# A two-layer hybrid decoder trunk on one core: the order of the first loads, weight splits and row factors

## The chip, the cores and the metric

The kernel runs on one core of a Trainium2 chip. A core has a matrix engine (TensorE, "PE" in the profile; its weight loads are listed apart as "PEld"), three engines for elementwise work (VectorE "DVE", ScalarE "ACT", GpSimd "POOL"), a queue engine (SyncE "SP") and 16 DMA engines that all queues share. Each engine runs its own list of instructions in the order in which the program was built; semaphores make one engine wait for another. The metric is the device time of one execution in microseconds, the median over runs. Lower is better.

## The reference

The input `x` has 256 rows of 1024 float32 values. Two layers follow each other; each adds half a SwiGLU, a token mixer and again half a SwiGLU, and a last norm closes:

```python
for layer in range(DEPTH):
    x = x + 0.5 * swiglu(rmsnorm(x, ffn1_norm[layer]), ffn1_w_gu[layer], ffn1_w_down[layer])
    h = rmsnorm(x, mix_norm[layer])
    y = gated_deltanet(h, ...) if layer % 2 == 0 else sliding_window_attention(h, ...)
    x = x + y
    x = x + 0.5 * swiglu(rmsnorm(x, ffn2_norm[layer]), ffn2_w_gu[layer], ffn2_w_down[layer])
return rmsnorm(x, final_norm)

def rmsnorm(x, w):
    return x * rsqrt(mean(x * x, axis=-1) + 1e-6) * w
def swiglu(h, w_gu, w_down):            # w_gu: 1024 x 5632, w_down: 2816 x 1024
    gate, up = split(h @ w_gu, 2)
    return (silu(gate) * up) @ w_down
```

## The kernel before

`x` stays on the chip as two row blocks of 128 rows (`t` = 0 and 1). The weights stream in from memory once, as float32, in pieces of 512 KB. float32 accuracy comes from three fast products: every operand is split into a high part with fewer bits and the rest. For a weight piece, `split` (L262) fetches `raw` on SP's queue, copies it into the reduced type on ACT (`whi`, L275), and subtracts that on DVE (`wlo`, L276). `mm3` (L306) then issues hi·hi, hi·lo and lo·hi; in the rows of the matrix engine these are L309 to L311. There are four buffers for `raw` and five each for `whi` and `wlo`, handed out in turn: the fifth `raw` can only be fetched when the first has been split, and the sixth `whi` can only be written when the products with the first are done.

`ffn` (L330) goes through the 2816 columns in eleven steps `c` of 256. Each step takes four pieces: two for the gate columns (`wg`: rows 0 to 511 and 512 to 1023 of `w_gu`) and two for the up columns (`wu`). A step has 4 products of 8 inner tiles each, so 96 matrix instructions. From step 1 on they are in the transposed form (`proj_T`), with both row blocks at once.

The very first norm is special (`First`, L125). The factor of a row, one over its root mean square, is not known when the first products could start. So the first step's products take `x * w` without the factor (`hh0`, `hl0`), one product for each row block, and the factor `r` is multiplied in behind (L372 to L374). `raw(t)` (L139) makes these operands: eight transposes of `x` on the matrix engine (`psT`, L149), a product with the norm's weights on DVE (`f`, L152), a copy of the high part on ACT (`hh`, L155) and a subtraction on DVE (`hl`, L156), in two halves `q` of four inner tiles. `factor(t)` (L159) takes squares and their sums on ACT (L164), and the power on POOL (L168). `scale()` (L172) spreads the factors over all partitions with two small products on the matrix engine (`prb<-dr,ones`, L177), copies the result on ACT (`rb`, L179), multiplies `f` by it on POOL in four parts (L183), and splits each part again (`hh` L185, `hl` L186). From step 1 on the products read these scaled operands.

Before the first data arrive, `warm` (L250) lets the matrix engine run products that nobody reads. After the transposes of row block 0, eight more of them follow (16 matrix instructions).

Three fetches go through ACT's queue at the start: `w8` (the first norm's weights, 4 KB), `nw` (the second norm's weights, spread over 128 partitions, 512 KB; used at the end of the first `ffn`) and `sk` (8 KB, used in the second layer). On SP's queue the order is: row block 0 of `x`, the two `wg` pieces, row block 1, the two `wu` pieces, and then the pieces of step 1 as buffers come free.

The order of instructions on each engine is not that of the Python code. A scheduler replays the program with estimated durations while it is built, and writes each engine's list in the order in which its instructions become ready there. `issue_after(ins)` tells it to put what follows behind `ins`. `hold` does that for the splits of a few weight pieces after a norm: their ACT and DVE instructions go behind the norm's last split.

## Time and profile before

| what | value |
|---|---|
| three runs | 1046.29, 1048.04, 1051.45 us; median 1048.04 us |
| span of the profiled execution | 1048.2 us |
| instructions in it | 18944 |
| read from memory | 174.92 MB, 168 GB/s over the span |
| DMA queue of SP: share of the 16 engines' time | 52.6% |
| ACT casts of weight pieces (L275) | 316, 1051 ns each on average |
| DVE subtractions of weight pieces (L276) | 302, 1268 ns each on average |

The profiled execution's own time, taken as its span, lies 0.2 us above the median of the three runs.

How to read the profile. A row of a timeline has the start in us, the time from the first to the last end of what is merged in it, the engine, the source line, the operation, `out<-in` by the program's names, the sizes and the count. In square brackets stand the idle time of the engine before it and what ended that. Matrix instructions are pipelined, so each lasts longer than the distance to the next start; the rate is read from starts. `PEclk` is the share of its full clock that the matrix engine was granted. The buffer numbers are left out of names in the profile, so `hh` can be `hh0` of the first step (L155) or the scaled `hh` (L185), and `w` is the norm's row `w8`.

### The profile page before, as it was taken

The numbers are of one execution on the slowest core, as the hardware profiler recorded it, in microseconds if no ns is written. First come the engines' busy times: TensorE is split into PE (matmuls) and PEld (weight loads), VectorE is DVE, ScalarE is ACT, GpSimd is POOL, SyncE is SP. The second block draws the span as 40 slices with busy tenths as digits, with TensorE's granted clock in tenths as the row PEclk, the third lists the DMA queues.
The fourth block names the chain that finished last, engine by engine and source line by source line (L and its number), as shares of the span: only waits on it lengthen the run. The fifth ranks groups of instructions, "written<-read, shape, count | busy, mean of one in ns | idle before, by whom it ended". The sixth has DMA issues, their size and how long they took to land.

```text
span 1048.2 us, 18944 instructions
## 1 busy us (share of the span) xinstructions
PE 1021.5 (97%) x7683; PEld 956.2 (91%) x7683; DVE 625.9 (60%) x887; ACT 498.8 (48%) x847; POOL 220.4 (21%) x197
## 2 busy tenths in 40 slices
PE   8999999999979999999999999999999999999997
PEld 7999998899979889999988999998899689999986
DVE  5755554666895665565545655554568856555544
ACT  5544443557755544443434433444456644344432
POOL 3123410006743201122100022120021401221100
PEclk9999999999989999999999999999999999999999
DMA  7666666654442335566565566567653426655661
GB/s 225 188 192 186 183 213 190 186 156 130 133 141 83 120 101 162 161 187 200 195 195 179 173 190 190 163 195 217 215 180 123 133 89 191 201 172 173 212 196 43
DMA packets 135003, 177.20 MB, mean 169 GB/s; under 512 B 6930, under 2 KB 119940, under 8 KB 134916
## 3 DMA queue, kind: packets, MB, share of 16 engines
q1 hardware_dynamic: 131712, 171.46, 52.6%
q10 hardware_dynamic: 3204, 4.53, 1.4%
q8 instruction: 60, 0.98, 0.4%
q14 instruction: 27, 0.22, 0.1%
HBM read 174.92 MB, written 1.05 MB: 168 GB/s over the span
## 4 chain that ended last, share of the span: by engine, by line
PE 62%; issue 1%; DVE 1%; ACT 0%; POOLq 0%; POOL 0%; ACTq 0%
PE acc L311 7%; PE acc L309 7%; PE acc L310 7%; PE pg L309 6%; PE pg L311 6%; PE pu L311 6%; PE pu L309 6%; PE pu L310 6%; PE pg L310 6%; PE pq L309 1%; PE pq L311 1%; PE pq L310 1%; PE psc L1103 1%; PE po L1147 1%; PE psT L89 1%
## 5 line engine op out<-in xcount | busy, mean ns | idle before, releaser
L275 ACT CAST whi<-raw 128x1024 fp32r<-128x1024 f32 x316 | 330.0, 1051 | 313.9 <-PE pg L310 161.5
L276 DVE TENSOR_TENSOR wlo<-raw,whi 128x1024 fp32r<-128x1024 f32 x302 | 382.1, 1268 | 154.3 <-ACT whi L275 153.8
L389 POOL TENSOR_SCALAR ah<-act 128x256 fp32r<-128x256 f32 x80 | 103.5, 1294 | 389.9 <-DVE act L340 389.9
L310 PE MATMUL pg<-hl,whi 128*128 128x256 f32 x640 | 181.2, 283 | 1.0 <-DVE hl L186 1.0
L310 PE MATMUL pu<-hl,whi 128*128 128x256 f32 x640 | 181.3, 283 | 0.0
L311 PE MATMUL pg<-hh,wlo 128*128 128x256 f32 x640 | 181.2, 283 | 0.0
L309 PE MATMUL pu<-hh,whi 128*128 128x256 f32 x640 | 181.2, 283 | 0.0
L311 PE MATMUL pu<-hh,wlo 128*128 128x256 f32 x640 | 181.2, 283 | 0.0
L309 PE MATMUL pg<-hh,whi 128*128 128x256 f32 x640 | 181.1, 283 | 0.0
L310 PE MATMUL acc<-wlo,ah 128*128 128x512 f32 (+1 forms) x340 | 128.4, 378 | 0.0
L311 PE MATMUL acc<-whi,al 128*128 128x512 f32 (+1 forms) x340 | 128.2, 377 | 0.0
L309 PE MATMUL acc<-whi,ah 128*128 128x512 f32 (+1 forms) x340 | 127.9, 378 | 0.0
L310 PEld LDWEIGHTS pg<-hl,whi 128*128 128x128 f32 x640 | 122.9, 192 | 1.2 <-DVE hl L186 1.2
L311 PEld LDWEIGHTS pg<-hh,wlo 128*128 128x128 f32 x640 | 122.9, 192 | 0.0
L309 PEld LDWEIGHTS pg<-hh,whi 128*128 128x128 f32 x640 | 122.9, 192 | 0.0
L311 PEld LDWEIGHTS pu<-hh,wlo 128*128 128x128 f32 x640 | 122.8, 192 | 0.0
L309 PEld LDWEIGHTS pu<-hh,whi 128*128 128x128 f32 x640 | 122.8, 192 | 0.0
L310 PEld LDWEIGHTS pu<-hl,whi 128*128 128x128 f32 x640 | 122.8, 192 | 0.0
L340 DVE TENSOR_TENSOR act<-sg,pu 128x256 f32<-128x256 f32 x86 | 35.9, 418 | 98.0 <-PE pu L311 96.2
L309 PEld LDWEIGHTS acc<-whi,ah 128*128 128x128 f32 x340 | 64.0, 188 | 11.9
L311 PEld LDWEIGHTS acc<-whi,al 128*128 128x128 f32 x340 | 63.9, 188 | 12.0
L310 PEld LDWEIGHTS acc<-wlo,ah 128*128 128x128 f32 x340 | 64.0, 188 | 11.7
(343 smaller groups left out, 1623.5 us busy)
## 6 DMA issues: line engine op xcount, KB each, us to landing
raw<-in_ffn_w_gu_dram SPq DMA_DIRECT2D x176, 512.0 KB, 4.9
raw<-in_ffn_w_down_dram SPq DMA_DIRECT2D x88, 512.0 KB, 4.3
raw<-in_a_w_in_dram SPq DMA_DIRECT2D x32, 512.0 KB, 4.5
raw<-in_b_w_in_dram SPq DMA_DIRECT2D x12, 512.0 KB, 4.9
raw<-in_a_w_out_dram SPq DMA_DIRECT2D x8, 512.0 KB, 3.9
raw<-in_b_w_out_dram SPq DMA_DIRECT2D x8, 512.0 KB, 3.8
nw<-in_ffn_norm_dram ACTq DMA_DIRECT2D x3, 512.0 KB, 4.1
x<-in_x_dram SPq DMA_DIRECT2D x2, 512.0 KB, 7.1
```

The lines of the kernel that those rows point to most:

```text
L89: last = nc.tensor.transpose(ps[:, i * P:(i + 1) * P], xn[:, s.start + i * P:s.start + (i + 1) * P], k.ident)
L275: nc.scalar.copy(hi, raw)
L276: (eng or nc.vector).tensor_tensor(out=lo, in0=raw, in1=hi.bitcast(F32), op=ALU.subtract)
L309: nc.tensor.matmul(out, lhsT=lh, rhs=rh, start=start, stop=False)
L310: nc.tensor.matmul(out, lhsT=lh, rhs=rl, start=False, stop=False)
L311: return nc.tensor.matmul(out, lhsT=ll, rhs=rh, start=False, stop=stop)
L340: ahead[1] = nc.vector.tensor_mul(a, sg, pu[:, :T])
L389: ahead[2] = nc.gpsimd.tensor_scalar(oh, a, 1.0, None, op0=ALU.mult)
L1103: nc.tensor.matmul(out, lhsT=qT[:, j, b * P:(b + 1) * P], rhs=kz[:, kv, :, kt * P:(kt + 1) * P], start=True, stop=True)
L1147: lastpo[0] = nc.tensor.matmul(po[64 * i:64 * i + 64, b * P:(b + 1) * P], lhsT=v[:, kt, kv * HD:(kv + 1) * HD], rhs=pT[:, b + kt, i, :], s ...
```

## The change

Five things are altered, all at the start of the program.

1. The second norm's weights (`nw`) are no longer fetched at the start, but at step 3 of the first `ffn`, behind the gate activation that is then the latest.
2. The two `wg` pieces of step 0 are loaded in two halves each (inner tiles 0-1 and 2-3 of a piece), and each half is split on its own: `cuts=2`.
3. `hold` is now also set by `raw(0)`: the splits of the two `wg` pieces go behind the last split of row block 0.
4. `raw(1)` is issued from within the loop over the first products, behind those of row block 0 with `wg`; the loop now runs over row blocks outside and halves of the inner tiles inside. `factor` and `scale` go behind the last split of row block 1.
5. The second group of unread products is six instead of eight (12 matrix instructions instead of 16).

```diff
 class Norm:
-    def __init__(self, kern, wrow):
+    def __init__(self, kern, wrow, later=False):
         self.k = kern
-        self.w = kern.n4([P, D], "nw")
-        kern.nc.scalar.dma_start(out=self.w, in_=wrow.partition_broadcast(P))
+        self.wrow = wrow
         self.hh = self.hl = None
+        if not later:
+            self.fetch()
+
+    def fetch(self):
+        self.w = self.k.n4([P, D], "nw")
+        self.k.nc.scalar.dma_start(out=self.w, in_=self.wrow.partition_broadcast(P))
...
 class First(Norm):
...
             oh = self.hh0[:, ks, ts]
-            nc.scalar.copy(oh, f)
-            nc.vector.tensor_sub(self.hl0[:, ks, ts], f, oh.bitcast(F32))
+            hi = nc.scalar.copy(oh, f)
+            lo = nc.vector.tensor_sub(self.hl0[:, ks, ts], f, oh.bitcast(F32))
+        if t == 0:
+            k.hold = [0, 2, hi, lo]
+        self.done = (hi, lo) if t else None
         return tr
...
-    def split(self, src, hi, lo, shape, eng=None):
+    def split(self, src, hi, lo, shape, eng=None, cuts=1):
         raw = self.wp.tile(shape, F32, tag="raw", name="raw", bufs=4)
-        nc.sync.dma_start(out=raw, in_=src)
+        n = shape[1] // cuts
+        parts = [slice(i * n, (i + 1) * n) for i in range(cuts)]
+        for c in parts:
+            nc.sync.dma_start(out=raw[:, c], in_=src[:, c])
...
-            nc.scalar.copy(hi, raw)
-            (eng or nc.vector).tensor_tensor(out=lo, in0=raw, in1=hi.bitcast(F32), op=ALU.subtract)
+            for c in parts:
+                nc.scalar.copy(hi[:, c], raw[:, c])
+                (eng or nc.vector).tensor_tensor(out=lo[:, c], in0=raw[:, c], in1=hi[:, c].bitcast(F32), op=ALU.subtract)
...
-            wg = self.wcols(w_gu, c * 256)
+            wg = self.wcols(w_gu, c * 256, cuts=2 if c == 0 and late is not None else 1)
             if c == 0 and late is not None:
                 late()
+            if c == 3 and fetch is not None:
+                with self.tc.issue_after(ahead[0].ins):
+                    fetch()
             wu = self.wcols(w_gu, DFF + c * 256)
...
                 for n, w in ((0, wg), (1, wu)):
-                    for ks in (range(0, 4), range(4, 8)):
-                        for t in range(NT):
-                            self.part_N(pgs[t][n][:, :T], w, t, nrm.hh0, nrm.hl0, ks)
-                for t in range(NT):
-                    nrm.factor(t)
-                nrm.scale()
+                    for t in range(NT):
+                        for ks in (range(0, 4), range(4, 8)):
+                            mm = self.part_N(pgs[t][n][:, :T], w, t, nrm.hh0, nrm.hl0, ks)
+                            if nrm.done is None:
+                                with self.tc.issue_after(mm.ins):
+                                    nrm.raw(1)
+                with ExitStack() as behind:
+                    for ins in nrm.done:
+                        behind.enter_context(self.tc.issue_after(ins.ins))
+                    for t in range(NT):
+                        nrm.factor(t)
+                    nrm.scale()
...
     with tc.issue_after(nrm.raw(0).ins):
-        K.warm(8)
+        K.warm(6)

     def late():
         load(1)
-        nrm.raw(1)
```

What the scheduler makes of it is seen in the lists of the engines, which name tiles with a number. First ACT at the start of the program, before. `hh0` is the high part of `x * w`; `whi_134` and `whi_140` are the `wg` pieces of step 0, `whi_163` and `whi_169` its `wu` pieces, and `whi_330` is the first piece of step 1.

```order
L275 CAST whi_134<-raw_136 128x1024
L155 CAST hh0_86<-f_85 128x4x128
L275 CAST whi_140<-raw_142 128x1024
L155 CAST hh0_86<-f_85 128x4x128
L164 ACTIVATE xn_284,ss_283<-x_81 128x512 x2
L275 CAST whi_163<-raw_165 128x1024
L155 CAST hh0_86<-f_85 128x4x128 x2
L275 CAST whi_169<-raw_171 128x1024
L179 COPY rb_298<-prb_291 128x256
L372 ACT_TABLE_LOAD
L372 ACTIVATE sg_312<-pg_175,r0_281 128x256
L275 CAST whi_330<-raw_332 128x1024
```

With the change ACT first makes both high parts of row block 0, then the four half pieces of `wg`, then the two `wu` pieces, and then come these rows. `whi_332`, `whi_338`, `whi_344` and `whi_350` are the four pieces of step 1, and `whi_468` is the first piece of step 2.

```order
L287 CAST whi_332<-raw_334 128x1024
L160 CAST hh0_86<-f_85 128x4x128 x2
L172 ACTIVATE xn_278,ss_277<-x_81 128x512 x2
L172 ACTIVATE xn_286,ss_285<-x_81 128x512 x2
L287 CAST whi_338<-raw_340 128x1024
L287 CAST whi_344<-raw_346 128x1024
L287 CAST whi_350<-raw_352 128x1024
L287 CAST whi_468<-raw_470 128x1024
L187 COPY rb_300<-prb_293 128x256
L394 ACT_TABLE_LOAD
L394 ACTIVATE sg_314<-pg_161,r0_283 128x256
L394 ACTIVATE sg_323<-pg_163,r1_291 128x256
```

The high parts of row block 1 stood behind three weight pieces; now they stand behind five, the last of them step 1's first. The copy of the spread factors (`rb`) stood behind step 0's last piece; now four pieces of step 1 and one of step 2 stand ahead of it too.

Second, the matrix engine behind the gate products of row block 0, before (`pg_175` is the gate product of row block 0 and `pg_177` that of row block 1; `pu_176` and `pu_178` are the up products):

```order
L311 MATMUL pg_175<-whi_140,hl0_87 128x256
L177 MATMUL prb_291<-dr_295,ones_75 128x128
L309 MATMUL pg_177<-whi_134,hh0_86 128x256
L310 MATMUL pg_177<-wlo_135,hh0_86 128x256
L309 MATMUL pu_176<-whi_163,hh0_86 128x256
```

And with the change, where `pg_161`, `pg_163` and `pu_162` have the same roles:

```order
L323 MATMUL pg_161<-whi_139,hl0_87 128x256
L321 MATMUL pg_163<-whi_130,hh0_86 128x256
L322 MATMUL pg_163<-wlo_131,hh0_86 128x256
L321 MATMUL pu_162<-whi_149,hh0_86 128x256
L322 MATMUL pu_162<-wlo_150,hh0_86 128x256
```

One of the two products that spread the factors (`prb`) is gone from here; in both lists two products of row block 1 stand ahead of the up products of row block 0. From the first of these two to the end of step 0 there are 72 products.

Third, the matrix engine at the end of step 0, before (`pg_354` is the first product of step 1):

```order
L309 MATMUL pu_178<-whi_169,hh0_86 128x256
L310 MATMUL pu_178<-wlo_170,hh0_86 128x256
L311 MATMUL pu_178<-whi_169,hl0_87 128x256
L309 MATMUL pg_354<-hh_88,whi_330 128x256
L310 MATMUL pg_354<-hl_89,whi_330 128x256
```

And with the change (`pu_164` is the last product of step 0, `pat` transposes step 0's result, `pg_356`, `pu_357`, `pg_412` and `pu_413` are the four products of step 1):

```order
L323 MATMUL pu_164<-whi_155,hl0_87 128x256
L185 MATMUL prb_293<-dr_294,ones_75 128x128
L185 MATMUL prb_293<-dr_297,ones_75 128x128
L400 MATMUL pat_318<-ident_70,act_316 128x128 x2
L321 MATMUL pg_356<-hh_88,whi_332 128x256
L321 MATMUL pu_357<-hh_88,whi_344 128x256
L321 MATMUL pg_412<-hh_88,whi_332 128x256
L400 MATMUL pat_327<-ident_70,act_325 128x128 x2
L321 MATMUL pu_413<-hh_88,whi_344 128x256
L322 MATMUL pg_356<-hl_89,whi_332 128x256
```

Both products that spread the factors now stand behind the last product of step 0, and the first transposes of its result ahead of step 1; before, step 1 followed step 0 directly and the transposes came in its middle. From there on the lists of all engines come to the same order within step 1 or 2, and nothing later differs but the one fetch of `nw` on ACT's queue at step 3.

More of the change, by code (lines that the diff above doesn't have):

```diff
@@ L325, in part_N, with ffn @@
             wh, wl = w(k, slice(0, 256))
-            self.mm3(out, hh[:, k, ts], hl[:, k, ts], wh, wl, k == 0, k == KT - 1)
-    def ffn(self, nrm, w_gu, w_down, after, mid=None, late=None, final=None):
+            mm = self.mm3(out, hh[:, k, ts], hl[:, k, ts], wh, wl, k == 0, k == KT - 1)
+        return mm
+    def ffn(self, nrm, w_gu, w_down, after, mid=None, late=None, final=None, fetch=None):
         nc = self.nc
```

13 lines of the change are left out of this document (7 added, 6 removed).

## The prediction

> **What bounds the kernel now.** I read the page first, then the matrix engine's waits, then the granted clock and the starts of the first 40 us. The page says that the matrix engine works almost without a break and that the chain that ends last runs on it.
>
> ```profile
> PE 1021.5 (97%) x7683; PEld 956.2 (91%) x7683; DVE 625.9 (60%) x887; ACT 498.8 (48%) x847; POOL 220.4 (21%) x197
> ...
> PE 62%; issue 1%; DVE 1%; ACT 0%; POOLq 0%; POOL 0%; ACTq 0%
> ```
>
> So the end moves by as much as the matrix engine's start of steady work moves. Its waits between 8 and 40 us are the first four rows here; the last row is the longest one from 40 to 280 us.
>
> ```profile
> PE pg L309 <- ACT hh L155: 1.2, 1, 1.2
> PE pg L310 <- DVE hl L186: 1.0, 1, 1.0
> PE pg L311 <- DVE hl L156: 0.8, 1, 0.8
> PE pg L310 <- DVE wlo L276: 0.4, 1, 0.4
> ...
> PE pvn L621 <- ACT vT L838: 0.5, 1, 0.5
> ```
>
> From 40 us on it waits for nothing longer than 0.5 us until the first mixer's tail, and the lists behind step 1 are the same in both versions. So I compare one point: the start of step 2. Its row, and those of the beginning:
>
> ```profile
> 10.96 0.39 PE L309 MATMUL pg<-whi,hh 128*128 128x256 f32 x1 [1.15 <-ACT hh L155]
> ...
> 27.04 0.28 PE L309 MATMUL pg<-hh,whi 128*128 128x256 f32 x1
> ...
> 29.00 0.39 PE L310 MATMUL pg<-hl,whi 128*128 128x256 f32 x1 [0.96 <-DVE hl L186]
> ...
> 34.72 0.28 PE L309 MATMUL pg<-hh,whi 128*128 128x256 f32 x1
> ...
> 40.48 0.28 PE L309 MATMUL pg<-hh,whi 128*128 128x256 f32 x1
> ```
>
> Step 0 ends and step 1 starts at 27.04; step 2 starts at 40.48. The 48 products from 34.72 to 40.48 give 0.12 us each. The clock (PEclk is the column with 1.00 or 0.50) is a second cost:
>
> ```profile
> 8.91:12.33 3.42, 1.67 (x10) 1.08 (x9) 1.91 (x3) 2.56 (x4) 0.00 (x0) 1.00 1.07 392
> 12.33:15.74 3.41, 2.84 (x13) 2.84 (x14) 2.37 (x4) 2.74 (x6) 0.55 (x1) 0.50 1.06 326
> 15.74:19.15 3.41, 3.41 (x30) 3.28 (x29) 3.05 (x5) 2.32 (x4) 0.00 (x0) 1.00 0.40 135
> ...
> 295.60:299.05 3.45, 0.00 (x0) 0.00 (x0) 3.45 (x5) 0.00 (x0) 1.34 (x2) 1.00 0.22 23
> 299.05:302.46 3.41, 1.06 (x5) 1.10 (x6) 3.41 (x9) 0.81 (x3) 0.00 (x0) 0.50 0.86 286
> 302.46:305.87 3.41, 3.41 (x18) 3.41 (x18) 3.41 (x7) 1.43 (x3) 0.47 (x1) 0.50 0.46 153
> ...
> 363.90:367.30 3.40, 1.58 (x14) 1.61 (x15) 2.23 (x10) 0.95 (x6) 1.91 (x2) 1.00 0.67 201
> 13.28 0.41 PE L309 MATMUL pg<-whi,hh 128*128 128x256 f32 x1
> 13.49 0.41 PE L310 MATMUL pg<-wlo,hh 128*128 128x256 f32 x1
> ```
>
> Stretches of 3.4 us are at half clock behind a stretch in which the engine was busy half the time or less (8.91 to 12.33, 295.60 to 302.46). A product then takes 0.21 us: each us at half clock loses 0.44.
>
> **The first products.** Row block 0 of `x` is there at 5.1:
>
> ```profile
> 5.11 0.63 ACT L164 ACTIVATE xn<-x 128x512 f32<-128x512 f32 x1 [1.54 <-DMA x<-in_x_dram]
> ...
> 5.13 1.97 PE L149 MATMUL psT<-ident,x 128*128 128x128 f32 x8 [0.40 <-DMA x<-in_x_dram]
> 6.89 2.91 PE L254 MATMUL warm<-ident 128*128 128x128 f32 x16
> ...
> 9.34 1.04 ACT L275 CAST whi<-raw 128x1024 fp32r<-128x1024 f32 x1 [2.90 <-DMA raw<-in_ffn_w_gu_dram]
> 10.29 0.61 ACT L155 CAST hh<-f 128x512 fp32r<-128x512 f32 x1
> 12.16 0.68 DVE L156 TENSOR_TENSOR hl<-f,hh 128x512 fp32r<-128x512 f32 x1
> ```
>
> Before, the high part of row block 0 stands behind a whole weight piece (9.34, 10.29). Now it goes first: transposes end at 7.1, `f` (0.68) at 7.8, `hh` (0.61) at 8.4, `hl` (0.68) at 9.1; the first half piece, cast as wide as `hh`, is split 8.4 to 9.0 on ACT, and 9.1 to 9.8 on DVE. So the gate products of row block 0 start at about 9.8 and, 24 of them with eight transposes of 0.11 between, end at 13.5. The first three waits above (2.4 us) go. The four unread instructions taken away end a stretch that ended at 9.8 at about 9.3, under this same wait: 0. The four half casts cost two extra starts, under 0.2 us, hidden by the next wait.
>
> **What is late next: row block 1.** Its `hh` stands on ACT behind step 1's first piece, and in the matrix engine's list two of its products stand ahead of the up products of row block 0, which therefore cannot fill the wait. When does that piece land? These rows are the issues of the first `wg` piece, of a `wu` piece and of step 1's first piece, and behind each its time to landing:
>
> ```profile
> 1.23 0.97 SPq L265 DMA_DIRECT2D raw<-in_ffn_w_gu_dram  x2
> raw<-in_ffn_w_gu_dram SPq DMA_DIRECT2D x1, 512.0 KB, 8.1
> 3.04 0.61 SPq L265 DMA_DIRECT2D raw<-in_ffn_w_gu_dram  x1
> raw<-in_ffn_w_gu_dram SPq DMA_DIRECT2D x1, 512.0 KB, 10.5
> 11.67 0.37 SPq L265 DMA_DIRECT2D raw<-in_ffn_w_gu_dram  x1
> raw<-in_ffn_w_gu_dram SPq DMA_DIRECT2D x1, 512.0 KB, 4.8
> ```
>
> They land at 9.3, 13.5 and 16.5. Two transfers of 512 KB fit in the last 3.0 us: 1.5 us each. Between the landing of `x` (5.1) and 9.3 are 4.2 us for one piece, so `nw` and `sk` together cost up to 2.7. I take 1.5 for `nw`, one transfer like the others, and leave `sk` its share, since it is still fetched there; the bounds are 0 and 2.7. With 1.5, step 1's first piece lands at 15.0. Its buffer allows that: both halves of the first piece are split at 10.4, where before the issue waited until 11.67. Its cast ends at 16.0, `hh` of row block 1 at 16.6 (its `f` is ready at 15.6, behind the split of a `wu` piece that lands at 12.0). So the matrix engine waits from 13.5 to 16.6, 3.1 us, a wait that before did not exist. Of 12.33 to 15.74 it is then busy a third, so I take half clock for 15.74 to 19.15: 2.5 us of work at a loss of 0.44, 1.1. The 72 products left take 8.6. Step 0 ends at 16.6 + 8.6 + 1.1 = 26.3, against 27.04: **-0.7**.
>
> The Trainium skill, "TensorE: Matmul & The Clock Gate", Part 1, puts the clock back to half only after at least one idle window of about 3.4 us. Here 8.91 to 12.33 was half busy, with no gap above 1.2 us, and half clock followed, so the row decides; by the page this loss of 1.1 would not come.
>
> **The scaling, now behind step 0.** These rows show the chain as it ran beside step 0's products:
>
> ```profile
> 17.95 1.05 ACT L275 CAST whi<-raw 128x1024 fp32r<-128x1024 f32 x1
> 18.90 0.36 ACT L179 COPY rb<-prb 128x256 f32<-128x256 f32 x1
> 19.28 1.28 ACT L372 ACT_TABLE_LOAD   x1
> 20.57 0.48 ACT L372 ACTIVATE sg<-pg,r 128x256 f32<-128x256 f32 x1
> L183 POOL TENSOR_TENSOR f<-f,rb x4: 1607/2013/2283, 19.5 to 25.5; 128x512 f32<-128x512 f32 x4
> ```
>
> With the change ACT casts step 2's first piece ahead of `rb`. That piece takes the buffer of step 0's last one, so the cast waits for step 0's last product, T. Then: cast from T+0.15, `rb` from T+1.1 (0.95 later, as from 17.95 to 18.90), the gate of row block 0 done at T+3.1 (2.05 after, as 18.90 to 20.95), that of row block 1 at T+3.5, and `hh` of step 1's first tiles (0.61) at T+4.1. POOL's first part starts at T+1.7 and at 1.6 to 2.3 us is ready by T+4.0, just in time. Step 1 starts at T+4.2. Its first four products and a transpose pair last 0.7, in which `hl` (0.68) is made. So step 2 starts at T + 4.2 + 0.3 + 96 x 0.12 = T+16.0, where before it was 40.48 - 27.04 = 13.4: **+2.6**. The idle 4.2 us also cost clock: half until the end of a 3.4 us stretch at about 32.8, with step 1 started at 30.5: 2.3 x 0.44 = **+1.0**.
>
> **Costs set to nothing.** The squares, sums and powers of the factor (2.5 us on ACT) move behind `hh` of row block 1, under the 72 products; without that cover they would add to the chain behind T. `nw` at step 3 adds a transfer of 1.5 us where the casts wait for the matrix engine and not for data; without that cover, 1.5. `sk` one place earlier on ACT's queue competes with `x` or the first half piece, 0 to 1.2, but ACT is busy with row block 0 until 8.4.
>
> **Sum.** -0.7 + 2.6 + 1.0 = +2.9 on the execution's own 1048.2 (0.2 above the median of the runs): 1051.1, so 1051. A measurement of this kernel can tell about 0.5% (5.2 us) from no change; the forecast is inside.
>
> **Rivals.**
>
> *The waits are shorter and the clock stays.* With 2.7 us for `nw` the piece lands at 13.8, but `f` of row block 1 bounds its `hh` to about 15.4: -1.2. The row at 363.90 shows full clock after a stretch busy 46%, so both losses (2.1) can fail to come. 1051.1 - 3.3 = 1047.8. Chance 0.17.
>
> *The fetch later brings nothing.* If `sk` and the number of transfers hold the queue rather than `nw`'s bytes, the piece lands at 16.5, 1.5 later: 1052.6. Against it: 4.2 us between two landings that elsewhere are 1.5 apart. Chance 0.10.
>
> *Slower: two stretches at half clock behind each wait*, as from 299.05 to 305.87, where even a stretch with work throughout was at half. Then 16.6 to 22.6 loses 2.6 instead of 1.1, and the stretch from step 1's start loses up to 2.5 instead of 1.0: +3.0, 1054.1. It decides from the point at which a stretch busy about 70% no longer brings the clock back; the row 12.33 to 15.74 (83%) did bring it back. Chance 0.13.
>
> *Slower: a half costs the queue what a whole piece costs.* Then step 1's first piece lands 2 x 1.5 later, 18.0, and the sum is 1054.1. Against it: transfers queued behind each other land as fast as their bytes. Chance 0.06. The Trainium skill, "DMA: Bandwidth & Descriptors", Rules for kernel authors, asks for at least 1 MiB per DMA and speaks against halves; no run here shows transfers of 256 KB.
>
> *Faster by over 0.5%* would need the waits at 13.5 and behind T both gone: 9.8 + 24 x 0.12 + 0.9 + 8.6 = 22.2 for the end of step 0, -4.8, and step 1 without its chain. The lists speak against it. Chance 0.05.
>
> **Chances and range.** The forecast has 0.49 and spans 1049 to 1053. With POOL at its slowest row (2.28 us a part) step 1's last tiles come late, +1.2. The range takes in the first two rivals with the runs' own spread below the median (1.75), and the slower rivals with POOL's bound: 1046 to 1055.5. Faster 0.05; slower 0.20 (the two slower rivals and a little of the forecast's edge); same 0.75.
>
> **What would show it.** Right: a wait of about 3 us of `pg` for `hh` (L160) near 13.5, a wait of about 4 us ahead of step 1, `rb` behind step 0's last product, half clock behind both, step 2 at about 43.3. Wrong: step 1 starting within 1 us of step 0's end, step 0 ending before 24, or the clock full throughout.

## The result and the profile after

| | before | after |
|---|---|---|
| median of six runs | 1048.53 us (1046.29 to 1051.45) | 1054.01 us (1052.15 to 1056.50) |
| span of the profiled execution | 1048.2 us | 1051.6 us |
| start of step 2 in it | 40.48 us | 45.51 us |

The ratio is 1.0054, with a 95% interval of 1.0037 to 1.0071: the kernel became slower by about 5.5 us. The forecast was 1051.0 us, the range 1046 to 1055.5.

Three values of a profiled execution have to be kept apart. Its time is 1.7 us more than its span (after: 1053.31 against 1051.6). The start of step 2 holds what the change itself does, +5.03 us. Between step 2 and the end of the last mixer 1.7 us come back, as the last rows of this section show.

The page first: matrix engine and chain are as before, its busy time even a little shorter. So the time was lost in waits and in the rate, not in more work.

```profile
PE 1020.9 (97%) x7679; PEld 955.5 (91%) x7679; DVE 624.2 (59%) x889; ACT 499.8 (48%) x849; POOL 217.6 (21%) x197
...
PE 62%; issue 1%; DVE 1%; ACT 0%; POOLq 0%; POOL 0%; ACTq 0%
```

The four longest waits of the matrix engine between 8 and 40 us (who waits, for whom, us in total, times, longest):

```profile
PE pg L321 <- ACT hh L160: 3.6, 1, 3.6
PE pat L400 <- DVE act L396: 3.3, 1, 3.3
PE pg L321 <- ACT whi L287: 0.8, 1, 0.8
PE pg L322 <- DVE wlo L288: 0.4, 1, 0.4
```

Before there were four short waits, 3.3 us together. Now there are two long ones, 6.9 us together, beside short ones. I call the long ones the first and the second wait. Their places, in the matrix engine's timeline, with the first product and the start of step 2:

```profile
8.03 0.39 PE L321 MATMUL pg<-whi,hh 128*128 128x256 f32 x1 [0.78 <-ACT whi L287]
...
12.90 0.28 PE L323 MATMUL pg<-whi,hl 128*128 128x256 f32 x1
16.77 0.58 PE L321 MATMUL pg<-whi,hh 128*128 128x256 f32 x1 [3.59 <-ACT hh L160]
...
27.78 0.61 PE L185 MATMUL prb<-dr,ones 128*128 128x128 f32 x4
...
31.66 0.44 PE L400 MATMUL pat<-ident,act 128*128 128x128 f32 x2 [3.27 <-DVE act L396]
...
32.15 0.52 PE L321 MATMUL pg<-hh,whi 128*128 128x256 f32 x1
...
45.51 0.28 PE L321 MATMUL pg<-hh,whi 128*128 128x256 f32 x1
```

The first product starts at 8.03 instead of 10.96. But step 0 ends (27.78, where `prb` stands) 0.74 later than before, step 1 starts 4.4 us behind that instead of at once, and it then takes longer. ACT's timeline says why each wait ends when it does:

```profile
15.15 1.04 ACT L287 CAST whi<-raw 128x1024 fp32r<-128x1024 f32 x1 [0.45 <-DMA raw<-in_ffn_w_gu_dram]
16.10 1.13 ACT L160 CAST hh<-f 128x512 fp32r<-128x512 f32 x2
...
27.98 1.04 ACT L287 CAST whi<-raw 128x1024 fp32r<-128x1024 f32 x1 [0.24 <-PE pu L323]
28.93 0.36 ACT L187 COPY rb<-prb 128x256 f32<-128x256 f32 x1
```

Row block 1's operand (`hh`, 16.10) stands behind step 1's first piece, which lands at 15.1. The copy of the factors (`rb`, 28.93) stands behind step 2's first piece, whose buffer is free only when step 0's last product is done.

The stretches by the granted clock (column with 1.00 or 0.50; the first number behind the comma is the time the matrix engine was busy):

```profile
11.77:15.18 3.41, 1.41 (x12) 1.21 (x11) 1.96 (x3) 2.12 (x3) 0.00 (x0) 1.00 1.09 346
15.18:18.60 3.42, 1.83 (x8) 1.83 (x9) 3.42 (x5) 3.42 (x8) 0.00 (x0) 0.50 0.76 226
18.60:22.01 3.41, 3.41 (x18) 3.41 (x17) 1.43 (x5) 1.10 (x4) 1.19 (x2) 0.50 0.82 263
22.01:25.42 3.41, 3.41 (x31) 3.41 (x30) 0.39 (x1) 1.05 (x1) 0.00 (x0) 1.00 0.06 16
...
28.84:32.25 3.41, 0.54 (x3) 0.30 (x3) 2.48 (x5) 3.32 (x7) 2.87 (x2) 1.00 0.86 267
32.25:35.66 3.41, 3.41 (x16) 3.41 (x17) 3.41 (x5) 1.87 (x4) 3.41 (x3) 0.50 0.72 242
```

Each wait leaves a stretch mostly empty (busy 41% and 16%), and half clock follows it: two stretches behind the first, one behind the second. A stretch in which the engine is busy throughout holds 18 or 16 matrix instructions at half clock and 31 at full.

What comes back in the middle. The first row of each pair is the mixer's first product of `pab`, the second the first output product of the last mixer; first of before, then of after:

```profile
212.29 0.33 PE L309 MATMUL pab<-hh,wabh 128*64 128x256 f32 x1 [0.24 <-ACT hh L92]
...
843.07 0.50 PE L309 MATMUL acc<-whi,oTh 128*128 128x512 f32 x1 [0.48 <-ACT oTh L1151]
```

```profile
217.32 0.33 PE L321 MATMUL pab<-hh,wabh 128*64 128x256 f32 x1 [0.24 <-ACT hh L97]
...
846.36 0.50 PE L321 MATMUL acc<-whi,oTh 128*128 128x512 f32 x1 [0.48 <-ACT oTh L1173]
```

The lead of before is 5.03 us at 212 and 3.29 at 843. In the first mixer the kernel before had one stretch at half clock more, from 316 to 319.5, which is 1.5 us at a loss of 0.44. Such later stretches come and go without any change to the kernel: a second profile of the changed kernel (e12) has two, from 370.80 to 374.21 and from 838.43 to 841.84, that the first has not. So I do not count this to the change, and the experiments are compared at the start of step 2.

### The profile page after: what moved, and what is told of

The parts are those of the page before. It is cut to its first block, busy times and chain, and to the rows that moved or that the text cites. A ratio compares the mean times of both kernels' runs of the same rounds, so it can differ in the third digit from the quotient of the medians.

```text
span 1051.6 us, 18945 instructions
## 1 busy us (share of the span) xinstructions
PE 1020.9 (97%) x7679; PEld 955.5 (91%) x7679; DVE 624.2 (59%) x889; ACT 499.8 (48%) x849; POOL 217.6 (21%) x197
## 4 chain that ended last, share of the span: by engine, by line
PE 62%; issue 1%; DVE 1%; ACT 0%; POOLq 0%; POOL 0%; ACTq 0%
PE acc L323 7%; PE acc L321 7%; PE acc L322 7%; PE pg L321 6%; PE pg L323 6%; PE pu L322 6%; PE pu L323 6%; PE pu L321 6%; PE pg L322 6%; PE pq L321 1%; PE pq L323 1%; PE pq L322 1%; PE psc L1125 1%; PE po L1169 1%; PE psT L94 1%
## 5 line engine op out<-in xcount | busy, mean ns | idle before, releaser
L287 ACT CAST whi<-raw 128x1024 fp32r<-128x1024 f32 (+1 forms) x318 | 330.2, 1046 | 317.8 <-PE pg L322 161.2
L288 DVE TENSOR_TENSOR wlo<-raw,whi 128x1024 fp32r<-128x1024 f32 (+1 forms) x304 | 378.7, 1250 | 157.4 <-ACT whi L287 157.1
```

What stands on the lines that cost most here:

```text
L287: nc.scalar.copy(hi[:, c], raw[:, c])
L288: (eng or nc.vector).tensor_tensor(out=lo[:, c], in0=raw[:, c], in1=hi[:, c].bitcast(F32), op=ALU.subtract)
```

## The experiments

My theory: the loss is in the two waits, which are made by the order of ACT's list, and in the slow clock behind them; the later fetch and the earlier first products are gains that the waits swallow. Rivals: the later fetch brings nothing; the halves cost the queue; the second wait has another cause; the clock is worth nothing.

| run | what it is | start of step 2 | half clock, 10 to 60 us | ratio to before, 95% interval |
|---|---|---|---|---|
| before | | 40.48 | 3.4 us | 1 |
| after | | 45.51 | 10.2 us | 1.0054 (1.0037 to 1.0071) |
| e1 | before, `nw` fetched later | 38.50 | 0 | 0.9990 (0.9979 to 1.0002) |
| e2 | after, factors not ordered | 36.04 | 0 | 0.9969 (0.9956 to 0.9981) |
| e3 | after, row block 1 early | 40.91 | 3.4 us | 1.0028 (1.0015 to 1.0042) |
| e4 | e2, and step 1's first piece behind row block 1 | 37.31 | 3.4 us | 0.9966 (0.9954 to 0.9979) |
| e5 | after, whole pieces | 44.13 | 7.6 us (up to 14.2, and behind the second wait) | 1.0051 (1.0031 to 1.0070) |
| e6 | after, waits overfilled | 45.69 | 0 | 1.0053 (1.0034 to 1.0071) |
| e7 | other order of the same parts | 36.96 | 0 | 0.9956 (0.9943 to 0.9969) |
| e8 | after, step 1's first piece behind row block 1 | 42.54 | 3.4 us | 1.0024 (1.0012 to 1.0036) |
| e9 | after, both waits filled | 41.95 | 0 | 1.0004 (0.9995 to 1.0013) |
| e10 | after, first wait filled | 43.60 | 3.4 us | 1.0025 (1.0012 to 1.0038) |

### e1: the later fetch alone

The edit of the kernel before, beside the new `fetch` that the change's own diff shows:

```diff
-        nxt = Norm(K, mix_norm[layer])
+        nxt = Norm(K, mix_norm[layer], later=layer == 0)
...
+            if c == 3 and fetch is not None:
+                with self.tc.issue_after(ahead[0].ins):
+                    fetch()
```

> The kernel before with one part of the change alone: the second norm's weights are fetched at step 3 and not at the start; nothing of the weights' pieces, the row blocks or the factors is changed. My theory (the fetch stood ahead of every later transfer, the change's loss is in the two waits and their slow clock): every piece lands about 1.4 us earlier, as in the changed kernel (step 1's first piece at 15.1 and not 16.5 us); the products of step 0 end 1.0 to 1.4 us earlier than 27.0, and step 2 starts at 39.1 to 39.5 and not at 40.5; no stretch at half clock in the beginning; the time is 1.2 us less, ratio 0.9989. Rival (the fetch was hidden, moving it brings nothing): step 2 at 40.5, ratio 1.000. Rival (the later fetch itself costs, where it lands at step 3): a wait in step 3 or 4 that the kernel before does not have, ratio over 1.001.

ACT's first cast of a weight piece in e1, which waited for the landing; before it stood at 9.34:

```profile
7.97 1.04 ACT L280 CAST whi<-raw 128x1024 fp32r<-128x1024 f32 x1 [2.26 <-DMA raw<-in_ffn_w_gu_dram]
```

The piece lands 1.37 us earlier, where the prediction took 1.5. Step 0 ends at 24.17, which is 2.87 earlier and more than I expected, since the stretch at half clock that the kernel before had from 12.33 to 15.74 did not come either (busy 83%, so it lost some 1.2 us). Step 1 then waits 1.9 us for the scaled operand's low part (`hl`), where it waited 1.0 before, and step 2 starts 1.98 earlier. The time alone, 1.0 us less, is not told apart from no change. The rival that the fetch was hidden falls by the profile: the cast's row is earlier and nothing at step 3 waits.

### e2: the factors not ordered

```diff
-                with ExitStack() as behind:
-                    for ins in nrm.done:
-                        behind.enter_context(self.tc.issue_after(ins.ins))
-                    for t in range(NT):
-                        nrm.factor(t)
-                    nrm.scale()
+                for t in range(NT):
+                    nrm.factor(t)
+                nrm.scale()
```

> The changed kernel with one order taken out: the rows' factors and the scaling of the operand no longer stand behind row block 1's operand, so the products of the factors' row stand early among step 0's and ScalarE's copy of them ahead of step 1's later pieces. My theory (the scaling chain that starts only at the end of step 0 is the second of two waits, and it brings the clock down): the wait of 3.3 us at 28.4 to 31.7 is gone or under 0.8 us, the half clock after it is gone, the wait for row block 1's operand at 13.2 us and its half clock stay within 1 us of what they are, step 2 starts at 40.0 to 41.0 and not at 45.5, ratio to the kernel before 0.9995 to 1.0005. Rival (the wait at the end of step 0 is set by something else, step 1's pieces or VectorE's load): step 2 stays at 45 to 45.5, ratio 1.005.

The two longest waits of the matrix engine in e2, 5 to 40 us, and four rows of ACT:

```profile
PE pg L321 <- ACT whi L287: 1.0, 1, 1.0
PE pg L321 <- ACT hh L160: 0.9, 1, 0.9
```

```profile
14.70 0.61 ACT L160 CAST hh<-f 128x512 fp32r<-128x512 f32 x1
15.22 1.04 ACT L287 CAST whi<-raw 128x1024 fp32r<-128x1024 f32 x1
16.17 0.62 ACT L160 CAST hh<-f 128x512 fp32r<-128x512 f32 x1
16.69 0.36 ACT L187 COPY rb<-prb 128x256 f32<-128x256 f32 x1
```

The second wait is gone, as expected: `rb` is copied at 16.69 and not at 28.93. But the first is down to 0.9 us as well, which I did not expect. With the factors free, the scheduler lays out ACT's list differently from the start: the squares go to its beginning, and the first half of row block 1's operand (14.70) comes ahead of step 1's first piece (15.22). So step 2 starts at 36.04 and not at 40 to 41. That each wait hangs on an edit of its own falls: the one order behind `nrm.done` makes the second wait, and without it the first is short too. It does not make the first alone, as e3 and e8 show, which keep it.

### e3: row block 1's transposes where they were

```diff
-                            if nrm.done is None:
-                                with self.tc.issue_after(mm.ins):
-                                    nrm.raw(1)
...
         load(1)
+        nrm.raw(1)
```

> The changed kernel with row block 1's transposes recorded where they were (with the load of x, ahead of the products); ScalarE makes its operand between the pieces of step 0 and ahead of step 1's first piece. The factors still stand behind it. My theory: the wait of 3.6 us at 13.2 us is gone or under 1.2 us, and of its two stretches at half clock at most one is left; step 0's products end at 24.5 to 26.0 and not at 27.8; the second wait stays, 4.2 to 4.4 us from the end of step 0 to step 1's first product, with a stretch at half clock behind it; step 2 starts at 42.2 to 43.7, ratio 1.0025 to 1.004. Rival (the first wait is set by the landing of the pieces, not by ScalarE's order): step 0 ends at 27 to 28, step 2 at 45 to 45.5, ratio 1.005.

```profile
PE pat L397 <- DVE act L393: 3.7, 1, 3.7
PE psT L154 <- DMA x<-in_x_dram: 2.3, 1, 2.3
```

The wait for row block 1's operand is gone; a shorter one, 2.3 us for row block 1 of `x` itself, takes its place ahead of the first products, since the transposes stand there in the list. Step 0 ends at 23.1 and step 2 starts at 40.91, both earlier than I expected, as no stretch at half clock is left behind the first products. The second wait stays, with half clock from 27.16 to 30.57. Taking the first wait away in this manner gains 4.6 us at step 2 (45.51 to 40.91). The time does not show all of it: step 2 starts 0.4 us behind the kernel before, and the median lies 2.6 behind. Beside the two at 300 us that both have, this profile has two later stretches at half clock (from 317.29 and from 832.71) where that of before has one; whether they account for the rest is not shown.

### e4: both taken on

The kernel of e2, and in `raw`:

```diff
         self.done = (hi, lo) if t else None
+        if t:
+            k.hold = [0, 1, hi, lo]
```

> The changed kernel with both waits taken on: the factors and the scaling free as in e2, and step 1's first piece ordered on ScalarE and VectorE behind row block 1's operand (the transposes stay where the change put them). My theory: the first wait shrinks from 3.6 to about 2 us and keeps one stretch at half clock (1.1 to 1.6 us lost), the second is gone, step 0 ends at 25 to 26.3 and step 2 starts at 37.2 to 38.8; ratio to the kernel before 0.997 to 0.9985. Rival (the change's halves and its later fetch bring nothing, and only the waits count): step 2 at 40 to 41, ratio 1.000. Rival (the clock costs as much whichever wait is left): step 2 at 39 to 40.

37.31 lies in the expected range, but not by the way that I expected: no wait for row block 1's operand is left, and all waits behind 13 us are 0.3 us or less. The wait of 2.0 us that is there is the one of the first product for `wg`. e2 starts step 2 1.27 us earlier. In both, the squares stand ahead of the first pieces and the first product starts late (9.31 in e2, 9.58 in e4). In e4 the matrix engine ran its transposes and unread products at full clock (8 transposes in 1.09 us, 1.97 in e2), was done sooner and waited longer (2.0 us against 1.0), and this stretch was followed by half clock, which fits the difference:

```profile
8.04:11.45 3.41, 1.45 (x10) 1.25 (x11) 3.32 (x6) 3.06 (x6) 0.00 (x0) 1.00 1.07 386
11.45:14.87 3.42, 3.42 (x19) 3.42 (x18) 2.45 (x7) 2.99 (x7) 0.55 (x1) 0.50 1.01 322
```

The times of e2 and e4 do not differ. The rival that the change brings nothing but the waits falls: both kernels are faster than the kernel before by 0.2 to 0.5%. Which of the other parts brings it, these two runs do not tell: the later fetch alone gives 0.1% (e1, not told apart from nothing), and row block 0 first and the fewer unread products were not run alone.

### e5: whole pieces

```diff
-            wg = self.wcols(w_gu, c * 256, cuts=2 if c == 0 and late is not None else 1)
+            wg = self.wcols(w_gu, c * 256, cuts=1)
```

> The changed kernel with the first two weight pieces loaded and split whole again. My theory (the halves start the first products about a microsecond earlier, but the first wait ends with row block 1's operand behind step 1's first piece and swallows it): the gate products of row block 0 end at 13.9 to 14.6 and not at 13.2, the wait behind them still ends at 16.6 to 16.9, step 2 starts at 45.2 to 45.8 as in the changed kernel (45.5); ratio 1.004 to 1.006. Rival (the halves cost queue time, whole pieces give it back): later pieces land over 0.3 us earlier, step 2 at 44.8 or less. Rival (the halves' microsecond reaches the end): step 2 at 46.3 to 46.8.

The ratio is that of the changed kernel (1.0051 against 1.0054, each with an interval of some 0.2% to either side), so no cost and no gain of the halves is seen at the end. The profile is no clean test: in this execution the full clock came only at 14.23, so the first products ran at half rate until then (their starts lie 0.21 us apart up to 13.1 and 0.12 from 14.8), and the wait behind them shrank to 1.2 us. That kept the next stretch busy (65%), no half clock followed, and step 2 started at 44.13, 1.4 us earlier than in the changed kernel's profile. This is in the range of the rival in which the halves cost queue time, but its reason is missing, since no piece lands earlier. ACT's row of step 1's first piece is at 15.19 here and at 15.15 with halves: two halves take the queue no longer than a whole piece.

### e6, e9 and e10: the waits filled with products that nobody reads

```diff
                                 with self.tc.issue_after(mm.ins):
                                     nrm.raw(1)
+                                    self.warm(15, self.psB("fill"))
...
-                    nrm.scale()
+                    pb = nrm.scale()
+                    with self.tc.issue_after(pb.ins):
+                        self.warm(12, self.psB("fill"))
```

e6 has 28 and 24 instead of 15 and 12; e10 has the first of the two only.

> The changed kernel with 28 products that nobody reads ahead of the first wait (between row block 1's transposes and row block 0's last gate products) and 24 behind the factors' row, in the second wait; nothing else is changed. My theory (part of the loss is not the waits but the slow clock behind them, 2.3 and 1.5 us, which follows TensorE's idle time): both waits still end where they did (16.8 and 31.7 to 32.2 less what step 0 gains), no stretch at half clock is left up to 60 us, step 0 ends 2.0 to 2.5 us earlier and step 2 starts at 41.3 to 42.3 and not at 45.5; ratio 1.0015 to 1.0025. Rival (the clock does not follow the idle time): the slow stretches stay, step 2 at 45 to 45.6. Rival (the fill delays what it stands before): step 2 over 45.6.

No half clock is left, but step 2 starts at 45.69. I had the fills too long: I took an unread product for 0.12 us, the rate of the others, and it takes 0.23. The two fills' rows in e6:

```profile
11.61 6.42 PE L262 MATMUL fill<-ident 128*128 128x128 f32 x56
28.38 5.52 PE L262 MATMUL fill<-ident 128*128 128x128 f32 x48
```

They are 2.8 and 2.2 us longer than the waits, and that ate what the clock gave, which is the second rival. By itself this could as well mean that the clock gives nothing, so:

> As e6, but with fills that fit into the waits: in e6 an unread product took 0.23 us (28 of them 6.42 us, 24 of them 5.52 us), so here 15 (3.4 us, against a wait of 3.6) and 12 (2.8 us, against 3.3). My theory (2.3 and 1.5 us of the loss are the slow clock behind the waits): no stretch at half clock up to 60 us, row block 1's products start at 16.5 to 17.3 and the second wait is where it was behind the end of step 0, step 0 ends at 25.3 to 26.3 and not at 27.8, step 2 starts at 41.5 to 42.6 and not at 45.5; ratio to the kernel before 1.001 to 1.0025. Rival (in e6 the fills cost exactly what the clock gave by chance, and the clock is worth nothing): 45 to 45.6, ratio 1.005. Rival (the waits themselves are shorter with a clock that is never slow, so both shrink further): under 41.2.

```profile
11.93 3.51 PE L262 MATMUL fill<-ident 128*128 128x128 f32 x30
...
25.35 0.61 PE L185 MATMUL prb<-dr,ones 128*128 128x128 f32 x4
25.80 2.84 PE L262 MATMUL fill<-ident 128*128 128x128 f32 x24
...
29.81 0.36 PE L321 MATMUL pg<-hh,whi 128*128 128x256 f32 x1
```

```profile
10.89:14.30 3.41, 3.41 (x33) 3.41 (x32) 1.73 (x3) 1.84 (x2) 0.00 (x0) 1.00 1.07 343
...
27.95:31.37 3.42, 2.45 (x19) 1.96 (x18) 2.58 (x6) 2.89 (x7) 3.42 (x3) 1.00 0.92 267
31.37:34.78 3.41, 3.41 (x31) 3.41 (x30) 3.13 (x4) 1.24 (x2) 2.25 (x2) 1.00 0.15 52
```

This is the clean cut. The second wait is as long as it was: step 1 starts 4.46 us behind step 0's end (25.35 to 29.81). Row block 1's products start at 16.7, as without the fill (16.77), so no useful work is ahead of where it was. Only the clock differs, and step 2 starts at 41.95: **3.56 us of the 5.03 are the slow clock.** The ratio falls from 1.0054 to 1.0004, a little more than expected: 0.50% are 5.2 us, which agrees with 3.56 only within the width of the two intervals (0.17% and 0.09% to either side).

> Only the first of e9's two fills (15 unread products ahead of the first wait). My theory (two stretches at half clock behind the first wait cost 2.3 us): neither is left, step 0 ends at 25.3 to 26.3, the second wait and its stretch at half clock stay, step 2 starts at 42.9 to 44.0; ratio 1.0025 to 1.004. Rival (one of the two stretches comes from the products' waits in step 0 and not from the first wait): one stretch is left, step 2 at 44.2 to 44.8.

In e10, the start of row block 1's products, the end of step 0 (`prb`) and the start of step 2:

```profile
17.04 0.39 PE L320 MATMUL pg<-whi,hh 128*128 128x256 f32 x1 [0.23 <-ACT hh L160]
...
25.78 0.61 PE L185 MATMUL prb<-dr,ones 128*128 128x128 f32 x4
...
43.60 0.28 PE L320 MATMUL pg<-hh,whi 128*128 128x256 f32 x1
```

No stretch at half clock is left behind the first wait, and step 2 starts at 43.60, as expected. But the start of step 2 does not split the 3.56 us rightly, since in this execution step 1's first piece is cast later (15.42) and row block 1's products start 0.3 us later than in the other two. Counted from their start to the end of step 0, the 72 products take 11.01 us in the changed kernel, 8.74 in e10 and 8.64 in e9: the slow clock behind the first wait costs 2.3 to 2.4 us. From the end of step 0 to step 2 it is 17.73 in the changed kernel, 17.82 in e10 and 16.60 in e9: the slow clock behind the second wait costs 1.1 to 1.2.

### e8: only the order of step 1's first piece

The changed kernel, and in `raw`:

```diff
         self.done = (hi, lo) if t else None
+        if t:
+            k.hold = [0, 1, hi, lo]
```

> The changed kernel with one order more: step 1's first piece is split behind row block 1's operand; the factors still stand behind that operand too. My theory (the first wait is long because step 1's first piece, landing at 15.1 us, stands ahead of row block 1's operand on ScalarE; the second is a wait of its own): the first wait ends at 15.2 to 16.0 and not at 16.8, at most one and a half stretches of slow clock remain, step 0 ends at 25.5 to 27.0, the second wait stays (step 1's first product 4.2 to 4.5 us behind the end of step 0), step 2 starts at 43 to 44.6; ratio 1.003 to 1.005. Rival (the operand itself is late, not its place): the first wait ends at 16.5 to 16.9 and step 2 starts at 45.2 to 45.6. Rival (freeing the first wait also frees the second): step 2 under 42.

```profile
PE pat L402 <- DVE act L398: 3.5, 1, 3.5
PE pg L323 <- ACT hh L160: 1.7, 1, 1.7
```

```profile
12.80:16.22 3.42, 1.71 (x15) 1.51 (x14) 3.29 (x4) 2.57 (x5) 0.00 (x0) 1.00 1.00 311
16.22:19.63 3.41, 3.41 (x30) 3.41 (x30) 2.01 (x6) 3.20 (x9) 1.11 (x2) 1.00 0.82 257
```

The first wait is half as long and ends at 15.46, and the second stays. So the first wait is long because step 1's first piece stands ahead on ACT. Step 2 starts at 42.54, 2.97 us earlier and a little more than expected: with the shorter wait the stretch stays busy 50%, and the clock stays full.

### e7: the same parts in another order

The kernel of e2, with the factors behind the last cast of `wg` (`cast`), with `wu` recorded behind `raw(1)`, and its second piece and step 1's first split behind row block 1's operand:

```diff
+                with self.tc.issue_after(cast.ins):
                     for t in range(NT):
                         nrm.factor(t)
...
+        if t:
+            k.hold = [1, 3, hi, lo]
```

> The change's parts in another order: later fetch, halves and row block 0 first are kept; the squares for the factors come behind the first weights' casts (not ahead of them as in e2 and e4, nor behind row block 1's operand), row block 1's operand ahead of the second of the up weights' pieces. My theory: first product at 8.0 to 8.2 (9.3 to 9.6 in e2 and e4), no wait over 1 us up to step 2, no slow clock, step 0 ends at 22.3 to 24.0, step 2 starts at 34.3 to 35.7; ratio to the kernel before 0.995 to 0.9965, 0.5 to 1 us below e2. Rival (GpSimd's four parts of the scaled operand set the start of step 1): waits for the scaled operand of 1 to 2 us inside step 1, step 2 at 36 to 37, no gain over e2.

Against the kernel before the ratio is 0.9956, the lowest of all, but its interval overlaps those of e2 and e4, so which of the three is best stays open. The first product starts at 8.66 (8.0 to 8.2 was expected), step 0 ends at 23.3, as expected, and step 2 starts at 36.96, later than expected and later than in e2. The rival that step 1 is held up by the scaling has the place right and the engine wrong. Step 1 waits 1.0 us at 25 us for a weight piece's low part from DVE, which is slow there. One row of GpSimd and three of DVE:

```profile
17.29 7.56 POOL L193 TENSOR_TENSOR f<-f,rb 128x512 f32<-128x512 f32 x4 [3.48 <-ACT rb L189]
```

```profile
19.97 2.03 DVE L290 TENSOR_TENSOR wlo<-raw,whi 128x1024 fp32r<-128x1024 f32 x1 [1.47 <-ACT whi L289]
...
23.62 2.31 DVE L290 TENSOR_TENSOR wlo<-raw,whi 128x1024 fp32r<-128x1024 f32 x1
...
27.85 1.21 DVE L290 TENSOR_TENSOR wlo<-raw,whi 128x1024 fp32r<-128x1024 f32 x1
```

### e11 and e12: both kernels again

Both are unchanged, each in one more profiled execution.

> The kernel before, unchanged, in a second profiled execution. The stretches after which the clock is set stand at another place in every execution. My theory (the first profiled execution of the kernel before had one stretch at half clock, 12.3 to 15.7 us, that other executions need not have, which is why its span and 1.7 us lie above the median of the runs): where no stretch at half clock falls between 10 and 40 us, step 2 starts at 39.1 to 39.5; where one falls into the first products again, at 40.2 to 40.8. The waits of 1.2, 0.8 and 1.0 us stay within 0.4 us. Rival (step 2 starts at the same time whatever the clock does, since the pieces' landings set it): 40.3 to 40.7 without any stretch at half clock.

> The changed kernel, unchanged, in a second profiled execution. My theory (each wait leaves a stretch nearly empty wherever the stretches lie, so the slow clock behind the second wait always comes; behind the first it depends on where they lie, 1 to 2 stretches or none): the waits are 3.2 to 3.8 and 3.1 to 3.6 us, step 2 starts at 45.3 to 45.7 with two slow stretches behind the first wait, 44.2 to 44.6 with one, 43.2 to 43.8 with none. Rival (the two losses are tied to each other, step 2 starts at the same time in each execution): 45.5 whatever the clock.

Before: step 2 at 40.54, again with one stretch at half clock among the first products (13.34 to 16.75), so the case without one did not come up and its rival stays open. The first of its waits is 2.5 us and not 1.2 as expected: the full clock came at 6.51 instead of 8.91, the unread products were done sooner, and the first product started where it had (10.94). After: step 2 at 45.88, 0.2 later than expected, waits of 3.5 and 3.3 us, again two stretches at half clock behind the first and one behind the second; whether step 2 moves with their number stays open. So the distance at step 2 is 5.0 us in one pair of profiles and 5.3 in the other, and the medians are 5.5 apart. The first of these rows is a stretch at half clock that was busy 73% and was followed by another at half:

```profile
15.81:19.23 3.42, 2.49 (x11) 2.50 (x12) 3.39 (x5) 3.42 (x10) 0.00 (x0) 0.50 0.80 239
19.23:22.64 3.41, 3.41 (x18) 3.41 (x17) 0.79 (x3) 0.44 (x2) 1.19 (x2) 0.50 0.70 213
```

## Where the prediction was right and where it was off

| step of the prediction | forecast | measured |
|---|---|---|
| gate products of row block 0 start | 9.8 | 8.03 |
| they end | 13.5 | 13.18 |
| step 1's first piece lands | 15.0 | 15.1 |
| products of row block 1 start | 16.6 | 16.77 |
| loss at half clock behind the first wait | 1.1 | 2.3 to 2.4 (11.01 us for 72 products, 8.74 and 8.64 in e10 and e9) |
| step 0 ends, against 27.04 | 26.3 (-0.7) | 27.78 (+0.74) |
| step 1 starts behind that | 4.2 | 4.37 |
| loss at half clock behind the second wait | 1.0 | 1.1 to 1.2 (e9 and e10) |
| step 2 starts | 43.3 (+2.9) | 45.51 (+5.03) |

**The mechanism was right.** Both waits came where the lists put them, for the reasons given, within 0.2 us of their ends. The later fetch was sized well (1.5 against 1.37 in e1). The halves were rightly set to nothing; the rival in which they cost the queue 3 us falls with step 1's first piece at 15.1. Of the four transfers of 256 KB in the profile after, the second and third land 0.7 us apart (7.9 and 8.6), half of the 1.5 of a whole piece. In part the end of the gate products was luck. They started 1.8 us earlier than forecast, as row block 0's transposes ended at 5.9 and not at 7.1 (1.16 us for the eight instead of 1.97), and lost 1.1 of it again where they waited for a low part of `wg` (8.03 to 8.85 for one product) and for row block 1 of `x` (10.14 to 10.66).

**The size of the clock term was off.** The forecast had 2.1 us for the half clock in both places; e9, which keeps the clock up and leaves the waits, gives 3.56. The term behind the second wait was right (1.0 against 1.1 to 1.2). The one that was too small is that behind the first (1.1 against 2.3 to 2.4). I assumed that one stretch at half clock follows a wait and that work in it lifts the clock. But the stretch into which the first wait reaches is itself part empty (54% busy in this profile, 73% in e12), and a second one at half followed. That is what the third rival described, with the point from which it decides, at about 70% busy. It came true behind the first wait and not behind the second, where the stretch was full; it had 0.13 for both. Its total, 1054.1, all but meets the measured median, but by chance: of the 3.0 us that it adds, about 1.5 came.

The Trainium skill, "TensorE: Matmul & The Clock Gate", Part 1, lets the clock fall back after at least one idle window of about 3.4 us and rise after a busy one, with windows that run free of the kernel. The last agrees: the stretches of 3.41 us lie elsewhere in each run. The first does not: the stretch from 11.77 to 15.18 was busy 41%, and half clock followed; by the page the loss behind the first wait would not have come, and e9 and e10 put it at 2.3 to 2.4 us.

**The rest.** None of the three signs named for a wrong forecast showed. Of the other rivals, shorter waits with a full clock did not come, and a later fetch that brings nothing falls by e1. The forecast stood on 1048.2, the span, taken as the time; the time lies 1.7 us above the span, so that execution's time would be 1049.9, 1.1 above the median of the 35 runs made beside e1 to e4 (1048.8). This shifts the base of the sum and not its terms. Of the 3.0 us between forecast and median, 2.2 are seen at the start of step 2: 1.3 for the clock behind the first wait, 0.2 for that behind the second, 0.3 for the ends of the two waits, and 0.3 in step 1 itself, which in e9 takes 12.1 us at full clock where the forecast had 11.8. For the other 0.8 no single cause is shown. The sum's highest case, the slower rivals with 1.2 for POOL, is 1055.3, where the range says 1055.5.

**What the sum did not see** is that one line takes part in both waits. The prediction treated the order of row block 1 and that of the factors as two edits with two prices. e2 takes back the second of them, and the second wait goes while the first shrinks to 0.9 us, since the scheduler lays the whole list out again. The first wait needs both orders: it also goes with the transposes of row block 1 recorded early (e3), and halves with step 1's first piece put behind row block 1 (e8). Without the two waits the change's other parts, taken together, are worth having: e2, e4 and e7 keep them and are 0.3 to 0.4% faster than the kernel before.

## What to carry to other kernels

An order that puts work "behind the operand that matters now" also puts it behind everything the list already holds there; look at what each engine's list has ahead of it, above all weights that have not landed and buffers that are not free. A wait on the matrix engine that leaves a stretch of the clock mostly empty cost here its own length and about half as much again (3.56 us beside waits of 6.9), so price it with two stretches at half clock where the wait reaches into the second; filling it with products that nobody reads, no longer than the wait, is a quick way to measure that part. Changes at a start are best compared at a fixed point soon behind them: there two profiles of the same kernel agreed within 0.4 us (40.48 and 40.54; 45.51 and 45.88), while later stretches of the clock move the end by more. The time of many runs still has the last word: in e3 it lay 2.2 us further behind than step 2.

## What the runs showed of the hardware that was not expected

- A stretch of 3.4 us at half clock does not lift the clock by being mostly busy: 54% (after) and 73% (e12) were followed by half, 83% (before, 12.33 to 15.74) by full. Over all fourteen profiles, every stretch at half clock that was busy 78% or less (e5, 304.37 to 307.78) was followed by half, and every one of 83% or more by full.
- At full clock no wholly idle stretch is needed for the fall: 16%, 41% and 49% were followed by half, and one of 50% by full (e8). Over all fourteen profiles, every stretch at full clock busy 41% or less was followed by half and every one above 65% by full. In between both came, so no sharp limit comes out of this: 43% in e3 (6.68 to 10.10) and 47% in before (363.90 to 367.31) were followed by full, 54% in before (312.70 to 316.11) and 65% in e8 (320.00 to 323.42) by half. The prediction's reading, half the time or less, was too narrow.
- DVE's subtraction of a weight piece takes 2.0 to 2.3 us while GpSimd multiplies, and 1.2 otherwise (e7). The Trainium skill, "GPSIMD Engine Reference", 1. Specifications, names the shared interface for instructions of VectorE with two operands in the on-chip memory, as this one has; the rows agree.
